# Rows of 1/rms by square root, reciprocal and a Newton step, in place of products with diagonals

## The chip, the cores and the metric

The kernel runs on one core of a Trainium2 chip. The metric is the device time of one execution in microseconds (us). A core has five engines that work at the same time, each through its own queue in order: TensorE (PE, matrix products, and PEld, its weight loads), VectorE (DVE), ScalarE (ACT, activation functions from tables), GpSimd (POOL) and SyncE (SP, which issues transfers). PE writes into PSUM, a memory of eight banks of 512 float32 columns on each of 128 partitions; DVE and ACT read PSUM and the on-chip memory SBUF.

## The reference

One encoder block on 512 tokens of width 1024, in float32. It has three mixers on the normalised input (a bidirectional mLSTM, a neighbourhood attention on a grid, a cross-attention into 256 memory tokens), merged by gates, and a gated convolutional FFN. What matters here is the RMS norm, which stands in three places ahead of products: on x, on mem, and ahead of the FFN.

```python
def rms_norm(x, g):
    xf = x.astype(F32)
    y = xf * lax.rsqrt(jnp.mean(xf * xf, axis=-1, keepdims=True) + EPS)
    return (y * g.astype(F32)).astype(x.dtype)
...
        h = rms_norm(x, mix_norm_g[l])
        proj = h @ w_in[l]
...
        mem_k, mem_v = jnp.split(rms_norm(mem, mem_norm_g[l]) @ w_mem_kv[l], 2, axis=-1)
...
    x = x + merged @ w_out[l]
    x = x + conv_glu_ffn(rms_norm(x, ffn_norm_g[l]), w_ffn_up[l], w_ffn_conv[l], b_ffn_conv[l], w_ffn_down[l])
    return rms_norm(x, final_norm_g)
```

## The kernel before

**Layout.** Activations lie with features on the 128 partitions and tokens along the columns: x is 8 tiles (KT) of 128 x 512. Each float32 operand of a large product is split into two parts of the faster type fp32r, a high part (a rounded copy, made on ACT) and a low part (the rest, made on DVE); a product is then three matmuls (`mm3`, L213 to L215: high by high, high by low, low by high). A projection (`proj`) is 8 x 3 matmuls of 512 columns into one PSUM bank.

**Weights.** They come from memory in blocks. `weights` keeps the transfers (L159, buffers `wr`) three blocks ahead and the splits one block ahead. A block is split in two halves; each has its high part on ACT (L195, `wh`) and its low part on DVE (L196, `wl`). There are four `wh` and four `wl` buffers, so a new half waits until PE has finished with the half four back.

**PSUM.** Two pools of four banks: `mm` for projections, `at` for all else. A projection into a fifth `mm` tile waits for a bank to be read out.

**The norm is applied late.** A projection multiplies the unnormalised input (with the gain g in it); its result is then scaled by 1/rms of each token. Where tokens lie along the columns, that takes a row: 1/rms of all tokens, the same on every partition (`rb`). Where tokens lie on the partitions, it takes a column (`rc`). Both come from the sums of squares: `acc` holds, on each partition, the squares added over the 8 tiles; `two_parts` (L301, L302) splits it; two products with a 128 x 128 tile of ones (L310) give the sum over all features on every partition, so the sums lie there as rows already.

- `rstd_cols` reads the sums with the diagonal of an identity, 128 columns at a time (L314), which gives a column, and takes the power -0.5 on POOL (L317).
- `rstd_row` makes the row from that column: `row_parts` splits the column in two parts (L324, L325) and multiplies the identity by each (L330, eight instructions on DVE for 512 tokens); two products of the ones with these diagonals (L339) spread the values over all partitions, and ACT copies them to `rb` (L341).

**Where they stand.** The order in the queues comes from the order of the code and from the Tile framework, which places the instructions of each engine.

1. *x.* Four projections for the queries (`ps_q`) fill the four `mm` banks; two for the keys (`ps_k`) use `at` banks. The sums and columns are made after the second step of the first key projection, the row after the fifth step of the second. The third key projection needs an `mm` bank; the first one is freed when `conv` has read it: L456 multiplies it by `rb` into `pad`, then follow three steps of a convolution (L458 on ACT, L459 and L460 on DVE) and a tanh (L465).
2. *mem* (256 tokens). Sums and columns after the second of four projections for the output gate (`o`), the row within the fourth. The code around it runs beside the mLSTM, whose steps are interleaved with the projections: Exps on ACT (L710, L714), products on DVE (L715, L717) that make the tiles E, matmuls with E (L725, L727), an Abs on ACT (L729), and gates on the projections (L1027, L1028).
3. *FFN.* The first two projections (`pa`, `pu`) are run up to their last step, which waits for the last tile; the sums stand between the last steps. Two more projections (`pa1`, `pu1`) follow; the row is made after the first step of `pu1`. Then `conv` reads `pa` with the row, and the next projection takes its bank.

Of the kernel before, what the change touches and what calls it, by code (L numbers as in the profile page):

```python
# [31 lines left out]
EPS = 1e-6  # L32
# [78 lines left out]
def hybrid_block(ctx, tc, xg, xT, memT, wflat, vecs, gbias, nabias, outa, outb, outc):  # L111
    nc = tc.nc
    V, A, G, PE, SY = nc.vector, nc.scalar, nc.gpsimd, nc.tensor, nc.sync
# [4 lines left out]
    sp = ctx.enter_context(tc.tile_pool(name="sp", bufs=7))  # L118
    tp = ctx.enter_context(tc.tile_pool(name="tp", bufs=2))
# [6 lines left out]
    def nm(s):  # L126
        uid[0] += 1
        return f"{s}_{uid[0]}"
# [13 lines left out]
    def atps():  # L142
        return atp.tile([P, 512], F32, tag="at", name=nm("at"))
# [4 lines left out]
    st = {"raw": 0, "split": 0}  # L148
# [122 lines left out]
    ident = cp.tile([P, P], F32, name="ident")  # L271
# [3 lines left out]
    onesr = cp.tile([P, P], F32R, name="onesr")  # L275
# [4 lines left out]
    for d in range(2):  # L280
        sgn = 1 if d == 0 else -1
        m = cp.tile([P, P], F32, name=f"msk{d}")
# [5 lines left out]
    for i in range(2):  # L288
        t = cp.tile([P, 514], F32, name=f"pad{i}")
# [9 lines left out]
    def two_parts(acc, ntok):  # L299
        h, l = [sp.tile([P, S], F32R, tag="scr", name=nm("s"))[:, :ntok] for _ in range(2)]  # L300
        A.activation(h, acc, AF.Copy)  # L301
        V.tensor_tensor(l, acc, h.bitcast(F32), op=ALU.subtract)  # L302
        return h, l

    def rstd_cols(parts, ntok, tag, n=D):

        nt = ntok // P
        ps = atps()
        for i in range(2):
            st["mm"] = PE.matmul(ps[:, :ntok], onesr, parts[i], start=i == 0, stop=i == 1).ins  # L310

        v, junk = tiny(nt), scr(P)
        for t in range(nt):
            V.tensor_tensor_reduce(junk, ps[:, t * P:(t + 1) * P], ident, 1.0 / n, EPS, ALU.mult, ALU.add,  # L314
                                   accum_out=v[:, t:t + 1])
        col = cp.tile([P, nt], F32, name=f"rc_{tag}")
        st["pool"] = G.tensor_tensor(col, v, nhalf[:, :nt], op=ALU.pow).ins  # L317
        return col

    def row_parts(col, ntok):  # L320

        nt = ntok // P
        ch, cl = tp.tile([P, 32], F32R, tag="tiny", name=nm("y"), bufs=12)[:, :nt], tiny(nt)
        A.activation(ch, col, AF.Copy)  # L324
        V.tensor_tensor(cl, col, ch.bitcast(F32), op=ALU.subtract)  # L325
        dgs = []
        for c in (ch.bitcast(F32), cl):
            dg = sp.tile([P, S], F32R, tag="scr", name=nm("s"))[:, :ntok]
            for t in range(nt):
                V.tensor_scalar(dg[:, t * P:(t + 1) * P], ident, c[:, t:t + 1], None, op0=ALU.mult)  # L330
            dgs.append(dg)
        return dgs

    def rstd_row(col, ntok, tag, parts=None):

        dgs = parts or row_parts(col, ntok)
        pb = atps()
        for n, dg in enumerate(dgs):
            PE.matmul(pb[:, :ntok], onesr, dg, start=n == 0, stop=n == 1)  # L339
        rb = cp.tile([P, ntok], F32, name=f"rb_{tag}", tag=f"rb{ntok}", bufs=1)  # L340
        A.activation(rb, pb[:, :ntok], AF.Copy)  # L341
        return rb


# [1 line left out]
    XH = [hx[k // 4 * 2][:, (k % 4) * S:(k % 4 + 1) * S] for k in range(KT)]  # L346
    XL = [hx[k // 4 * 2 + 1][:, (k % 4) * S:(k % 4 + 1) * S] for k in range(KT)]
# [3 lines left out]
    ps_k = [atps() for _ in range(2)]  # L351
# [35 lines left out]
    norm = []  # L387
# [7 lines left out]
    def proj(key, XHs, XLs, n=S, at={}, ps=None):  # L395

        ws = weights(key)
        k0 = 0 if ps is None else 1
        if ps is None:
            ps = mmps()  # L400
        for k in range(k0, KT):
            mm3(ps[:, :n], ws[k][0], ws[k][1], XHs[k], XLs[k], k == 0, k == KT - 1)
            if k == 1:
                flush()
            if k in at:
                at[k]()
        return ps
# [32 lines left out]
                mm3(ps_k[f], kh[:, fs], kl[:, fs], XH[0], XL[0], True, False)  # L440

    xsum = two_parts(acc, S)
    proj(("mlk", 0), XH, XL, ps=ps_k[0], at={1: lambda: norm.append(rstd_cols(xsum, S, "x"))})
    proj(("mlk", 1), XH, XL, ps=ps_k[1], at={4: lambda: norm.append(rstd_row(norm[0], S, "x"))})
    rc, rb = norm
    SY.dma_start(gbf, gbias.partition_broadcast(P))
    rcc = cp.tile([P, NT], F32, name="rcc")
    V.tensor_scalar(rcc, rc, C_ML, None, op0=ALU.mult)
# [22 lines left out]
    for f in range(4):  # L471
        ps = ps_k[f] if f < 2 else proj(("mlk", f), XH, XL)
# [27 lines left out]
    for c in range(3):  # L500
        n, nk = TMC[c], TMK[c]
        pss = [(mmps if c % 2 else atps)() for _ in range(NT)]
        for h in range(KT // nk):
            ws = weights(("tm", c, h))
            for t in range(NT):
                tsl = slice(t * P, (t + 1) * P)
                for k in range(nk):
                    kk = nk * h + k
                    ps = pss[t][:, :n]
                    mm3(ps, XH[kk][:, tsl], XL[kk][:, tsl], ws[k][0], ws[k][1], kk == 0, kk == KT - 1)  # L510
        for t in range(NT):
            ps = pss[t]
            if c == 0:
                V.scalar_tensor_tensor(Gt[:, t, :], ps[:, :16], rc[:, t:t + 1], gb, op0=ALU.mult, op1=ALU.add)
            if c < 2:
                o = 16 if c == 0 else 0
# [494 lines left out]
    gens.append(ml_all())  # L1011

    xq = unit()
    mrbs = []
    for f in range(4):
        ps = proj(("xaq", f), XH, XL)
        V.tensor_tensor(xq[:, f * S:(f + 1) * S], ps, rb, op=ALU.mult)
        mem_part(f)
        step(RB)
    for f in range(4):  # L1020
        def mem_row():
            with tc.issue_after(st["mm"]):
                mrbs.append(rstd_row(mrc, M, "m", mparts))

        ps = proj(("o", f), XH, XL, at={1: mem_row} if f == 3 else {})
        t = scr()
        V.tensor_tensor(t, ps, rb, op=ALU.mult)  # L1027
        A.activation(t, t, AF.Tanh, scale=0.5)  # L1028
        if f == 0:
            so.append(unit())  # L1030
            msum = two_parts(macc, M)
        if f == 1:

            with tc.issue_after(st["mm"]):
                mrc = rstd_cols(msum, M, "m")
        if f == 2:
            mparts = row_parts(mrc, M)
        V.tensor_scalar(so[0][:, f * S:(f + 1) * S], t, 1.0, None, op0=ALU.add)
        step(RB)
    mrb = mrbs[0]  # L1040
    mkv = unit()
    mk, mv = mkv[:, 0:1024], mkv[:, 1024:2048]
    for f in range(4):
# [245 lines left out]
    for hh in range(2):  # L1289
        gu = [unit(F32R) for _ in range(6)]  # L1290
        UH = [gu[k // 4][:, (k % 4) * S:(k % 4 + 1) * S] for k in range(HF)]
        UL = [gu[3 + k // 4][:, (k % 4) * S:(k % 4 + 1) * S] for k in range(HF)]
        for j in range(HF):
            f = HF * hh + j
            if f == 0:
                wa, wu = weights(("ua", f)), weights(("uu", f))
                pa, pu = mmps(), mmps()
                for k in range(KT):
                    if k < KT - 1:
                        mm3(pa, wa[k][0], wa[k][1], HH[k], HL[k], k == 0, False)  # L1300
                for k in range(KT - 1):
                    mm3(pu, wu[k][0], wu[k][1], HH[k], HL[k], k == 0, False)
                k = KT - 1
                mm3(pa, wa[k][0], wa[k][1], HH[k], HL[k], False, True)
                rc2 = rstd_cols(two_parts(acc2, S), S, "2")
                mm3(pu, wu[k][0], wu[k][1], HH[k], HL[k], False, True)
                pa1 = proj(("ua", 1), HH, HL)
                norm2 = []
                pu1 = proj(("uu", 1), HH, HL, at={0: lambda: norm2.append(rstd_row(rc2, S, "2"))})
                rb2 = norm2[0]  # L1310
            else:
                pa = pa1 if f == 1 else proj(("ua", f), HH, HL)
            c = conv(pa, rb2, "ffw", "ffb", f, FT)
            sq = scr()
            A.activation(sq, c, AF.Square)
            V.scalar_tensor_tensor(sq, sq, GC, c, op0=ALU.add, op1=ALU.mult)  # L1316
            A.activation(sq, sq, AF.Tanh, scale=GK)  # L1317
            V.scalar_tensor_tensor(c, sq, 1.0, c, op0=ALU.add, op1=ALU.mult)  # L1318
            G.tensor_tensor(c, c, rb2, op=ALU.mult)  # L1319
            if f > 0:  # L1320
                pu = pu1 if f == 1 else proj(("uu", f), HH, HL)
            V.tensor_tensor(c, pu, c, op=ALU.mult)  # L1322
            split_act(UH[j], UL[j], c, 0.5)
        for f in range(KT if hh == 0 else LF - 1):
            ws = weights(("dn", hh, f, 0)) + weights(("dn", hh, f, 1))
            ps = mmps()
            for k in range(HF):
                mm3(ps, ws[k][0], ws[k][1], UH[k], UL[k], k == 0, k == HF - 1)
            V.tensor_tensor(x2[f], ps, x2[f], op=ALU.add)
            if hh == 1:  # L1330
                if f == 0:
                    A.activation(acc3, x2[f], AF.Square)
                else:
                    sq = scr()
                    A.activation(sq, x2[f], AF.Square)
                    G.tensor_tensor(acc3, acc3, sq, op=ALU.add)
# [117 lines left out]
```

## Time and profile before

| | |
|---|---|
| device time, 3 runs | 878.7, 879.12, 879.23 us; median 879.12 |
| profiled execution: span from the first to the last instruction | 878.1 us |
| median of the runs less that span | 1.0 us |
| PE busy | 872.7 us (99%) |
| DVE busy | 582.2 us (66%) |
| ACT busy | 451.4 us (51%) |
| POOL busy | 127.1 us (14%) |
| read from memory, written | 94.80 MB, 4.21 MB |

The profile gives no device time of its own for the profiled execution, only the span. In its lines, "L456 DVE TENSOR_TENSOR pad<-mm,rb_x 128x512 ... x6 | 4.1, 689 | 0.7" names the line of the code, the engine, the operation, the tiles written and read, the shape and the count; then the busy time in us, the mean of one in ns, and the idle time of the engine just before, with what ended it behind an arrow. A timeline has the start and the length in us ahead of these. Matmuls overlap: their listed length runs to the modelled end, and the next one starts earlier. "PEclk" is the clock granted to PE in tenths.

### The profile page before, as it was taken

Reading aid. Unit: us, or ns where it says so; the run is one execution under the profiler, and the core shown is the slowest. Engines: PE = TensorE matmul, PEld = TensorE weight load, DVE = VectorE, ACT = ScalarE, POOL = GpSimd, SP = SyncE. Lnnn points to the kernel's source line nnn. Section 1 sums busy time; section 2 is a strip of 40 time slices with the busy share of each in tenths; the row PEclk is TensorE's granted clock in tenths of the full one; section 3 lists DMA queues with packets and bytes.
Section 4 is the critical chain, followed back from the end, with each engine's and each line's share of the span. In section 5 each row is a group of like instructions: output and inputs, shape, how many; then the busy total and the mean of one; then the engine's idle time right before and its main releaser. Section 6 shows DMA issues by size and latency. Waiting matters only on the chain.

```text
span 878.1 us, 12238 instructions
## 1 busy us (share of the span) xinstructions
PE 872.7 (99%) x4334; PEld 740.4 (84%) x4334; DVE 582.2 (66%) x1211; ACT 451.4 (51%) x953; POOL 127.1 (14%) x203
## 2 busy tenths in 40 slices
PE   9999999999999999999999999999999999999997
PEld 7898889888888888888888888888888888888897
DVE  7694686775667758898676558776633466666433
ACT  7363555754456658888544435444422344444532
POOL 0101100001072460700000002111100011111011
PEclk9999999999999999999999999999999999999999
DMA  8224643522242354533223432222233322222412
GB/s 280 99 73 140 207 135 97 192 85 90 74 137 87 107 146 131 156 110 130 97 97 109 144 107 94 99 97 96 72 103 101 109 97 97 98 97 87 141 34 96
DMA packets 39421, 99.81 MB, mean 114 GB/s; under 512 B 5688, under 2 KB 13880, under 8 KB 39360
## 3 DMA queue, kind: packets, MB, share of 16 engines
q1 hardware_dynamic: 31568, 92.32, 31.1%
q0 software_dynamic: 7360, 6.32, 3.1%
q8 instruction: 34, 0.56, 0.3%
q10 hardware_dynamic: 432, 0.39, 0.1%
q14 instruction: 27, 0.22, 0.1%
HBM read 94.80 MB, written 4.21 MB: 113 GB/s over the span
## 4 chain that ended last, share of the span: by engine, by line
PE 99%; issue 0%; ACT 0%; DVE 0%; POOLq 0%; POOL 0%; DVEq 0%
PE mm L213 29%; PE mm L215 29%; PE mm L214 29%; PE at L214 2%; PE at L213 2%; PE at L215 2%; PE at L872 1%; PE at L725 1%; PE at L853 1%; PE at L727 1%; PE at L690 1%; PE at L834 0%; PE at L835 0%; PE at L706 0%; PE at L960 0%
## 5 line engine op out<-in xcount | busy, mean ns | idle before, releaser
L213 PE MATMUL mm<-u,wh 128*128 128x512 f32 (+1 forms) x1072 | 415.6, 388 | 0.0
L215 PE MATMUL mm<-u,wl 128*128 128x512 f32 (+1 forms) x1072 | 412.2, 385 | 0.0
L214 PE MATMUL mm<-u,wh 128*128 128x512 f32 (+1 forms) x1072 | 411.8, 384 | 0.0
L195 ACT ACTIVATE wh<-wr 128x512 fp32r<-128x512 f32 (+2 forms) x298 | 184.1, 622 | 234.4 <-PE mm L214 188.1
L196 DVE TENSOR_TENSOR wl<-wr,wh 128x512 fp32r<-128x512 f32 (+3 forms) x300 | 203.1, 678 | 92.4 <-ACT wh L195 85.8
L215 PEld LDWEIGHTS mm<-u,wl 128*128 128x128 f32 x1072 | 201.5, 188 | 40.1
L214 PEld LDWEIGHTS mm<-u,wh 128*128 128x128 f32 x1072 | 201.8, 188 | 38.8
L213 PEld LDWEIGHTS mm<-u,wh 128*128 128x128 f32 x1072 | 201.8, 188 | 38.2
L1319 POOL TENSOR_TENSOR s<-s,rb 128x512 f32<-128x512 f32 x22 | 38.3, 1739 | 250.0 <-DVE s L1318 238.1
L538 POOL DMA_DIRECT2D u<-nav_d x128 | 62.2, 512 | 66.5 <-PE at L872 22.5
L219 ACT ACTIVATE u<-s 128x512 fp32r<-128x512 f32 x26 | 16.4, 630 | 57.5 <-DVE s L1322 56.1
L1322 DVE TENSOR_TENSOR s<-mm,s 128x512 f32<-128x512 f32 x22 | 15.2, 691 | 25.1 <-POOL s L1319 25.1
L458 ACT ACTIVATE s<-pad,vec 128x512 f32<-128x512 f32 x30 | 24.4, 813 | 9.5 <-DVE pad L456 9.5
L459 DVE SCALAR_TENSOR_TENSOR s<-pad,vec,s 128x512 f32<-128x512 f32 x30 | 23.6, 786 | 6.1 <-ACT s L458 6.0
L220 DVE SCALAR_TENSOR_TENSOR u<-s,u 128x512 fp32r<-128x512 f32 x26 | 18.0, 691 | 14.1 <-ACT u L219 14.0
L1318 DVE SCALAR_TENSOR_TENSOR s<-s,s 128x512 f32<-128x512 f32 x22 | 15.2, 692 | 13.4 <-ACT s L1317 13.3
L317 POOL TENSOR_TENSOR rc<-y,nhalf 128x4 f32<-128x4 f32 x1 | 1.0, 1032 | 152.9 <-DVE y L314 152.9
L460 DVE SCALAR_TENSOR_TENSOR s<-pad,vec,s 128x512 f32<-128x512 f32 x30 | 22.5, 750 | 0.7
L1317 ACT ACTIVATE s<-s 128x512 f32<-128x512 f32 x22 | 13.9, 632 | 15.1 <-DVE s L1316 15.1
L456 DVE TENSOR_TENSOR pad<-mm,rb 128x512 f32<-128x512 f32 x22 | 15.1, 691 | 7.3 <-PE mm L215 6.5
L213 PE MATMUL mm<-wh,u 128*128 128x512 f32 x48 | 18.9, 394 | 0.0
L214 PE MATMUL mm<-wl,u 128*128 128x512 f32 x48 | 18.8, 392 | 0.0
(315 smaller groups left out, 1028.4 us busy)
## 6 DMA issues: line engine op xcount, KB each, us to landing
wr<-wflat SPq DMA_DIRECT2D x141, 512.0 KB, 3.3
nab<-nabias SPq DMA_DIRECT2D x16, 256.0 KB, 2.7
u<-nav_d POOLq DMA_DIRECT2D x128, 32.0 KB, 2.6
s<-xT SPq DMA_DIRECT2D x15, 256.0 KB, 3.9
wr<-wflat SPq DMA_DIRECT2D x14, 192.0 KB, 2.3
nav_d<-nv POOLq DMA_DIRECT2D x8, 256.0 KB, 2.4
R<-rd SPq DMA_DIRECT2D x8, 256.0 KB, 3.9
wr<-wflat SPq DMA_DIRECT2D x2, 544.0 KB, 3.3
```

The lines of the kernel that those rows point to most:

```text
L195: A.activation(h[:, u:v], src, AF.Copy)
L196: V.tensor_tensor(l[:, u:v], src, h[:, u:v].bitcast(F32), op=ALU.subtract)
L213: PE.matmul(ps, lh, rh, start=start, stop=False)
L214: PE.matmul(ps, lh, rl, start=False, stop=False)
L215: st["mm"] = PE.matmul(ps, ll, rh, start=False, stop=stop).ins
L219: A.activation(h, src, AF.Copy, scale=scale)
L220: V.scalar_tensor_tensor(l, src, scale, h.bitcast(F32), op0=ALU.mult, op1=ALU.subtract)
L458: A.activation(t1, pad[:, 0:512], AF.Identity, scale=vcol(w, i), bias=vcol(b, i))
L459: V.scalar_tensor_tensor(t1, pad[:, 1:513], vcol(w, n + i), t1, op0=ALU.mult, op1=ALU.add)
L460: V.scalar_tensor_tensor(t1, pad[:, 2:514], vcol(w, 2 * n + i), t1, op0=ALU.mult, op1=ALU.add)
L538: G.dma_start(vw[r * 32:(r + 1) * 32, i * 256:(i + 1) * 256], nav_v[hf, r, CW[b]:CW[b] + 32, hp * 256:(hp + 1) * 256])
L1319: G.tensor_tensor(c, c, rb2, op=ALU.mult)
```

## The change

`rstd_cols` is parted: `square_sums` makes the sums by the two products with ones and leaves them in PSUM, and `rstd_cols` takes the column from there as before. `rstd_row` no longer uses the column. It works on the sums themselves, which lie on all partitions: v = sum / n + eps, s = sqrt(v) on ACT, y = 1 / s on DVE, and one Newton step y (1.5 - 0.5 v y y) in three instructions on DVE. The diagonals, their two products and the copy are gone in all three places. The row stands right behind the sums, ahead of the column where one is made; in the FFN no column is made any more.

```diff
-    def rstd_cols(parts, ntok, tag, n=D):
-
-        nt = ntok // P
+    def square_sums(parts, ntok):
+
         ps = atps()
         for i in range(2):
             st["mm"] = PE.matmul(ps[:, :ntok], onesr, parts[i], start=i == 0, stop=i == 1).ins
-
+        return ps
+
+    def rstd_cols(ps, ntok, tag, n=D):
+
+        nt = ntok // P
         v, junk = tiny(nt), scr(P)
...
-    def row_parts(col, ntok):
-
-        nt = ntok // P
-        ch, cl = tp.tile([P, 32], F32R, tag="tiny", name=nm("y"), bufs=12)[:, :nt], tiny(nt)
-        A.activation(ch, col, AF.Copy)
-        V.tensor_tensor(cl, col, ch.bitcast(F32), op=ALU.subtract)
-        dgs = []
-        for c in (ch.bitcast(F32), cl):
-            dg = sp.tile([P, S], F32R, tag="scr", name=nm("s"))[:, :ntok]
-            for t in range(nt):
-                V.tensor_scalar(dg[:, t * P:(t + 1) * P], ident, c[:, t:t + 1], None, op0=ALU.mult)
-            dgs.append(dg)
-        return dgs
-
-    def rstd_row(col, ntok, tag, parts=None):
-
-        dgs = parts or row_parts(col, ntok)
-        pb = atps()
-        for n, dg in enumerate(dgs):
-            PE.matmul(pb[:, :ntok], onesr, dg, start=n == 0, stop=n == 1)
+    def rstd_row(ps, ntok, tag, n=D):
+
+        v, s = scr(ntok), scr(ntok)
         rb = cp.tile([P, ntok], F32, name=f"rb_{tag}", tag=f"rb{ntok}", bufs=1)
-        A.activation(rb, pb[:, :ntok], AF.Copy)
+        V.tensor_scalar(v, ps[:, :ntok], 1.0 / n, EPS, op0=ALU.mult, op1=ALU.add)
+        A.activation(s, v, AF.Sqrt)
+        V.reciprocal(rb, s)
+        V.tensor_tensor(v, v, rb, op=ALU.mult)
+        V.scalar_tensor_tensor(v, v, -0.5, rb, op0=ALU.mult, op1=ALU.mult)
+        V.scalar_tensor_tensor(rb, v, 1.5, rb, op0=ALU.add, op1=ALU.mult)
         return rb
...
-    proj(("mlk", 0), XH, XL, ps=ps_k[0], at={1: lambda: norm.append(rstd_cols(xsum, S, "x"))})
-    proj(("mlk", 1), XH, XL, ps=ps_k[1], at={4: lambda: norm.append(rstd_row(norm[0], S, "x"))})
-    rc, rb = norm
+    def x_norm():
+        ps = square_sums(xsum, S)
+        norm.extend([rstd_row(ps, S, "x"), rstd_cols(ps, S, "x")])
+
+    proj(("mlk", 0), XH, XL, ps=ps_k[0], at={1: x_norm})
+    proj(("mlk", 1), XH, XL, ps=ps_k[1])
+    rb, rc = norm
...
-        def mem_row():
-            with tc.issue_after(st["mm"]):
-                mrbs.append(rstd_row(mrc, M, "m", mparts))
-
-        ps = proj(("o", f), XH, XL, at={1: mem_row} if f == 3 else {})
+        ps = proj(("o", f), XH, XL)
...
             with tc.issue_after(st["mm"]):
-                mrc = rstd_cols(msum, M, "m")
-        if f == 2:
-            mparts = row_parts(mrc, M)
+                mps = square_sums(msum, M)
+            mrb, mrc = rstd_row(mps, M, "m"), rstd_cols(mps, M, "m")
...
-                rc2 = rstd_cols(two_parts(acc2, S), S, "2")
+                rb2 = rstd_row(square_sums(two_parts(acc2, S), S), S, "2")
                 mm3(pu, wu[k][0], wu[k][1], HH[k], HL[k], False, True)
                 pa1 = proj(("ua", 1), HH, HL)
-                norm2 = []
-                pu1 = proj(("uu", 1), HH, HL, at={0: lambda: norm2.append(rstd_row(rc2, S, "2"))})
-                rb2 = norm2[0]
+                pu1 = proj(("uu", 1), HH, HL)
```

More of the change, by code (lines that the diff above doesn't have):

```diff
@@ L1013, in hybrid_block @@
     xq = unit()
-    mrbs = []
     for f in range(4):
@@ L1034, in hybrid_block @@
             with tc.issue_after(st["mm"]):
-                mrc = rstd_cols(msum, M, "m")
-        if f == 2:
-            mparts = row_parts(mrc, M)
+                mps = square_sums(msum, M)
+            mrb, mrc = rstd_row(mps, M, "m"), rstd_cols(mps, M, "m")
         V.tensor_scalar(so[0][:, f * S:(f + 1) * S], t, 1.0, None, op0=ALU.add)
         step(RB)
-    mrb = mrbs[0]
     mkv = unit()
```

## The prediction

> **What bounds the kernel now.** I read the page first: the share of each engine, the granted clock by slice and the chain that ended last.
>
> ```profile
> span 878.1 us, 12238 instructions
> ...
> PE 872.7 (99%) x4334; PEld 740.4 (84%) x4334; DVE 582.2 (66%) x1211; ACT 451.4 (51%) x953; POOL 127.1 (14%) x203
> ...
> PEclk9999999999999999999999999999999999999999
> ...
> PE 99%; issue 0%; ACT 0%; DVE 0%; POOLq 0%; POOL 0%; DVEq 0%
> ```
>
> TensorE (PE) is busy 99% at full clock, and the chain of work that ended last is PE for 99%. Then the waits of PE alone, whose only entry is the start of the program:
>
> ```profile
> PE at L243 <- PEq L1441: 0.8, 1, 0.8
> ```
>
> So a matmul taken away shortens the span by its place in PE's stream, and a wait put in front of PE lengthens it one for one: no later idle time is there to take it back. What a place is worth, and how near PE already is to a wait, shows the timeline around the first row of 1/rms (rb_x):
>
> ```profile
> 36.38 0.62 PE L339 MATMUL at<-s,onesr 128*128 128x512 f32 x2
> 37.03 0.60 ACT L341 ACTIVATE rb_x<-at 128x512 f32<-128x512 f32 x1 [0.73 <-PE at L339]
> 37.66 1.29 DVE L456 TENSOR_TENSOR pad<-mm,rb_x 128x512 f32<-128x512 f32 x2 [0.63 <-ACT rb_x L341]
> 38.42 0.39 PE L214 MATMUL at<-u,wh 128*128 128x512 f32 x1
> 38.65 0.39 PE L215 MATMUL at<-u,wl 128*128 128x512 f32 x1
> 38.65 0.19 PEld L213 LDWEIGHTS mm<-u,wh 128*128 128x128 f32 x1
> 38.88 0.39 PE L213 MATMUL mm<-u,wh 128*128 128x512 f32 x1
> ```
>
> Matmuls of 512 columns start 0.227 us apart (38.42, 38.65, 38.88), though each is listed with 0.39. The first matmul into a new mm bank starts at 38.88. All four mm banks hold q projections until then, and the first is freed by the first "pad" of L456, at 37.66 + 0.69 = 38.35, which needs rb_x. The cover is 0.3 us at the weight load.
>
> **The change part by part.**
>
> *PE, removed:* in each of three places two products with the diagonals (L339).
>
> ```profile
> 139.00 0.40 PE L339 MATMUL at<-s,onesr 128*128 128x256 f32 x2
> ...
> L339 PE MATMUL at<-s,onesr 128*128 128x512 f32 x4 | 1.2, 389 | 0.0
> L339 PE MATMUL at<-s,onesr 128*128 128x256 f32 x2 | 0.4, 280 | 0.0
> ```
>
> Four of 512 columns at 0.227 make 0.91. Two of 256 span 0.40 with 0.28 for one, so they start 0.12 apart: 0.24. Together −1.14 us. The sums themselves (L310) stay.
>
> *New work on the row:* v from PSUM, a square root on ACT, a reciprocal, three Newton steps on DVE. The built program also has six more table loads on ACT, one before each square root and one before the next Tanh or Exp. Nearest rows:
>
> ```profile
> L267 ACT ACT_TABLE_LOAD x1 | 1.3, 1283 | 1.7 <-PEq L1441 1.7
> L465 ACT ACTIVATE s<-s 128x512 f32<-128x512 f32 x8 | 5.0, 629 | 6.3 <-DVE s L460 6.1
> L732 DVE RECIPROCAL y<-y 128x2 f32<-128x2 f32 x16 | 2.6, 163 | 0.3
> L556 DVE RECIPROCAL y<-y 128x32 f32<-128x32 f32 x1 | 0.4, 355 | 0.0
> L456 DVE TENSOR_TENSOR pad<-mm,rb_x 128x512 f32<-128x512 f32 x6 | 4.1, 689 | 0.7 <-ACT rb_x L341 0.6
> ```
>
> v and each Newton step: 0.69, and two such in a row start 0.60 apart (1.29 for the two pads). Root: 0.63. The reciprocal of 512 is nowhere shown. Below: 0.69, as any other elementwise pass. Above: 355/32 = 11.1 ns a column, so 5.68. I take the line through the two rows, (355 − 163)/30 = 6.4 ns a column: 0.163 + 510 × 0.0064 = 3.43, and 1.79 for 256, because it keeps the fixed part that the row of two columns shows.
>
> [...]
>
> *First place (x).* Times are those of before; DVE and ACT take their queues in order.
>
> ```profile
> 29.13 0.62 PE L310 MATMUL at<-s,onesr 128*128 128x512 f32 x2
> ...
> 29.90 0.29 DVE L314 CUSTOM_DVE_ANT_0 s<-at,ident 128x128 f32<-128x128 f32 x1
> ...
> 31.29 1.03 POOL L317 TENSOR_TENSOR rc_x<-y,nhalf 128x4 f32<-128x4 f32 x1 [28.75 <-DVE y L314]
> ...
> 32.35 0.84 DVE L448 TENSOR_SCALAR rcc<-rc_x 128x4 f32<-128x4 f32 x1 [1.15 <-POOL rc_x L317]
> 32.46 0.73 DVE L196 TENSOR_TENSOR wl<-wr,wh 128x512 fp32r<-128x512 f32 x1
> ...
> 39.11 0.62 ACT L195 ACTIVATE wh<-wr 128x512 fp32r<-128x512 f32 x1
> ```
>
> v takes the place of the first reduction: 29.90 to 30.59. The table load waits for v: 30.62 to 31.90; root to 32.56. Meanwhile the reductions and the power of the columns come 0.60 later, so rcc leaves the head of DVE's queue at 33.06, and the reciprocal runs 33.06 to 36.49. Behind it the built program has, on DVE: split of a weight (L196), Newton 1, split, Newton 2, split, Newton 3, split, pad. At 0.60 apart from 36.42 the pad starts at 40.62 and ends at 41.31. PE without its two products would want the bank at 38.43; it gets it at 41.4 and first loads 0.19 of weights, so its matmul starts at 41.6. Stall 3.2 us, in place of a cover of 0.3.
>
> What else stands behind the new waits: on ACT, behind the root, the high halves of two weight splits. The first ran at 30.96 before (it waits for PE's buffers) and now runs at 32.6 to 33.2, in time for its low half, which DVE can take only after the reciprocal anyway (36.42 to 37.1) and which PE wants after 38.9. On POOL, behind the power, only the clearing of mLSTM tiles, 0.6 later and wanted tens of microseconds on. SP's queue isn't passed by anything.
>
> What is late next: PE is 3.2 − 0.45 = 2.75 later than before. The pads are 2.96 later, but a split that stood behind them (0.60) is done already, so DVE is 2.4 later and closes up; the Tanh load fits the 1.56 us that ACT idled before its first Tanh:
>
> ```profile
> 41.29 0.63 ACT L465 ACTIVATE s<-s 128x512 f32<-128x512 f32 x1 [1.56 <-DVE s L460]
> ```
>
> Bounds. With a reciprocal of 5.68 the stall is 3.2 + 2.25 = 5.4. With 0.69 it doesn't vanish: the last split before the pad needs its high half from ACT, whose buffer PE frees only with the last but one matmul of the projection (38.42 above, 37.97 without the products, +0.39 = 38.36). Then 0.63 on ACT (in before it ran at 39.11), 0.60 for the split, 0.69 for the pad, 0.25 to the matmul: 40.6, a stall of 2.2 at least.
>
> *Third place (FFN).* It has more cover:
>
> ```profile
> 519.34 0.63 ACT L195 ACTIVATE wh<-wr 128x512 fp32r<-128x512 f32 x1 [2.03 <-PE mm L214]
> 520.53 0.63 ACT L195 ACTIVATE wh<-wr 128x512 fp32r<-128x512 f32 x1 [0.56 <-PE mm L214]
> ...
> 520.61 0.28 DVE L314 CUSTOM_DVE_ANT_0 s<-at,ident 128x128 f32<-128x128 f32 x1
> ...
> 527.90 1.29 DVE L456 TENSOR_TENSOR pad<-mm,rb 128x512 f32<-128x512 f32 x2 [0.63 <-ACT rb L341]
> ...
> 531.83 0.39 PE L213 MATMUL mm<-u,wh 128*128 128x512 f32 x1
> ```
>
> The next bank is wanted at 531.83, 531.38 without the products. v 520.61 to 521.30; load behind the split of 520.53, to 522.45; root 523.08; reciprocal 526.54; split, Newton, split, Newton, Newton, split, pad end at 530.9, PE could start at 531.1. Stall 0, cover 0.3; with 5.68 it is 2.0. The weights of the projection that runs meanwhile are split before the reciprocal.
>
> *Second place (memory, 256 columns).* No conv waits on this row, but ACT and DVE feed the mLSTM there.
>
> ```profile
> 143.54 0.69 DVE L1027 TENSOR_TENSOR s<-mm,rb_x 128x512 f32<-128x512 f32 x1 [1.54 <-PE mm L215]
> 144.15 0.41 DVE L715 TENSOR_TENSOR E<-E,at 128x256 f32<-128x256 f32 x1
> ...
> 145.11 0.39 PE L725 MATMUL at<-u,E 128*128 128x129 f32 x2
> ```
>
> Before, the E of 144.15 is ready at 144.56 for PE at 145.11. Now ACT loads the root's table after the tanh that ended at 133.70 and has the root (0.38) at 135.3; the reciprocal keeps DVE until 137.1, which moves weight splits by 1.6 that PE wants only after 143. The load for the next Exp stands in ACT's queue right behind the Abs of a chunk (L729, 138.20 before), which waits for PE's products of 137.40 to 137.79 and runs at 137.9. The load is done at 139.3, and the Exps that began at 138.25 begin a good 1.0 later. With the rest of ACT's queue E's factors are complete at about 142; a split and the product of L1027 (143.6) stand ahead of E on DVE, which has it at 144.6. PE's own queue, shorter by 0.24, wants it at 144.85: stall 0, cover 0.2. A reciprocal of 2.84 (256 × 11.1 ns) moves only what is ready before 142 and the last products by up to 1.05: stall 0.9 at most.
>
> ```profile
> 133.07 0.63 ACT L1028 ACTIVATE s<-s 128x512 f32<-128x512 f32 x1 [1.59 <-DVE s L1027]
> ...
> 137.40 0.39 PE L727 MATMUL at<-u,E 128*128 128x129 f32 x2
> 138.20 0.15 ACT L729 ACTIVATE y<-at 128x2 f32<-128x2 f32 x1
> 138.25 0.69 ACT L710 ACTIVATE E<-R,bi 128x128 f32<-128x128 f32 x2
> ...
> 139.43 0.38 ACT L341 ACTIVATE rb_m<-at 128x256 f32<-128x256 f32 x1
> ```
>
> Priced at nothing: the diagonals and small products taken from DVE (L330, L325) and the copies from ACT (L341, L324), because neither engine sets the end there; they are in the walks as room in the queues. The columns of the third place, which aren't made any more, are of that kind too.
>
> **The sum.** −1.14 + 3.2 + 0 + 0 = +2.06 on the span of 878.1: 880.2. The runs shown have a median of 879.12, 1.0 above this span; the time forecast is 879.12 + 2.06 = 881.2. Bounds: −1.14 + 2.2 = +1.06 (880.2) and −1.14 + 5.4 + 2.0 + 0.9 = +7.2 (886.3).
>
> **The rivals.**
> 1. *A short reciprocal, the split as the bound.* If it costs 0.69 to 2.2, the wait for the last weight split decides: 880.2. Against it: both rows of reciprocals grow with columns far beyond what a split does.
> 2. *A table switch that costs more than its load.* The only load in the trace stands at the start, with no activation before it to be finished. If a switch took a second 1.28: first place +0.8 (0.5 of it is hidden behind rcc), third +1.0 beyond its cover, second 2 × 1.28 − 0.2 = +2.3; 881.2 + 4.1 = 885.3. For it: six switches at places with covers of 0.2 to 0.5. [...] Long reciprocals end in the same region.
> 3. *No stall: not slower.* The row is ready before the bank is wanted, so only the six matmuls count: 879.12 − 1.14 = 878.0. It decides if the pad's end comes before 38.2, that is over 3 us earlier than the walk gives and 2.2 before the split that stands ahead of it allows. It holds only if DVE's order on the chip is another than the built one, for which nothing speaks.
>
> **How the numbers follow.** Forecast 0.55 (own range 880.7 to 882.2), rival 1 0.20, rival 2 with long reciprocals 0.20, rival 3 0.05. About 0.2% (1.76 us, to 880.9) can be told from no change. The forecast lies just above that: I put 0.09 of its 0.55 below. Slower 0.46 + 0.20 + 0.02 of rival 1 = 0.68; even rival 3 is only 0.13% faster, so faster 0.02 and within 0.2% the remaining 0.30. The range leaves out most of rival 3 and the upper tail: 879.9 to 885.6.
>
> **What would show it.** In the changed profile: a wait of PE for DVE's pad near 41 us, of about 3.2, and none near 145 and 531; a reciprocal of 512 near 3.4 us; ACT_TABLE_LOAD seven times 1.28, with the square root right behind; PE records down by six. Wrong if PE waits nowhere, if the wait is near 2.2 with a short reciprocal (rival 1), or if waits stand at all three places (rival 2).

## The result, and the profile after

| | before | after |
|---|---|---|
| device time, median of 5 runs | 879.23 us (878.7 to 879.63) | 883.33 us (882.0 to 883.44) |
| ratio, with its 95% interval | | 1.0041 (1.0029 to 1.0053) |
| profiled execution, span | 878.1 us | 881.6 us |

The changed kernel is slower by 0.4%, 4.1 us. Its five runs fall apart into two kinds: three with spans of 881.6 to 881.7 and a mean granted clock of 0.997 or 0.998 (883.33 to 883.44), and two with spans of 880.2 and 880.3 and a clock of 1.0 (882.0 and 882.07). The profiled execution is of the first kind.

The page after: the span, the busy time of the engines, and the chain that ended last, by engine.

```profile
span 881.6 us, 12217 instructions
...
PE 873.2 (99%) x4328; PEld 740.2 (84%) x4328; DVE 592.5 (67%) x1195; ACT 457.7 (52%) x956; POOL 126.3 (14%) x202
...
PE 95%; DVE 3%; issue 1%; ACT 0%; POOL 0%; POOLq 0%; DVEq 0%
```

Six matmuls fewer (4334 to 4328), and yet PE is busy 0.5 us longer; the chain has 3% of DVE in it, where before it was PE alone. PE's waits, in total, times and longest, say where:

```profile
PE mm L213 <- DVE pad L451: 2.5, 1, 2.5
PE at L243 <- PEq L1427: 0.8, 1, 0.8
PE mm L215 <- DVE wl L196: 0.5, 1, 0.5
```

The wait for the first pad at x was forecast. The wait for the low half of a weight split was not. The timeline of ACT, DVE and PE around x (start, length, engine, line):

```profile
30.45 1.28 ACT L328 ACT_TABLE_LOAD   x1 [1.51 <-DVE s L327]
31.74 0.63 ACT L328 ACTIVATE s<-s 128x512 f32<-128x512 f32 x1
...
32.72 0.38 DVE L443 TENSOR_SCALAR rcc<-rc_x 128x4 f32<-128x4 f32 x1 [1.15 <-POOL rc_x L320]
32.80 3.35 DVE L329 RECIPROCAL rb_x<-s 128x512 f32<-128x512 f32 x1
36.06 0.63 DVE L196 TENSOR_TENSOR wl<-wr,wh 128x512 fp32r<-128x512 f32 x1
...
39.61 0.68 DVE L196 TENSOR_TENSOR wl<-wr,wh 128x512 fp32r<-128x512 f32 x1
40.21 1.28 DVE L451 TENSOR_TENSOR pad<-mm,rb_x 128x512 f32<-128x512 f32 x2
...
38.13 0.39 PE L215 MATMUL at<-u,wl 128*128 128x512 f32 x1
41.04 0.76 PE L213 MATMUL mm<-u,wh 128*128 128x512 f32 x1 [2.52 <-DVE pad L451]
41.60 0.63 PE L214 MATMUL mm<-u,wh 128*128 128x512 f32 x1
42.03 0.63 PE L215 MATMUL mm<-u,wl 128*128 128x512 f32 x1
```

The walk is the forecast one: load, root, reciprocal behind rcc, four splits with the three Newton steps between them, pads. PE would have gone on at 38.13 + 0.227 = 38.36 and goes on at 41.04, a stall of 2.68. But then its matmuls start 0.43 apart (41.60, 42.03) in place of 0.227, and are listed with 0.63. Busy time and granted clock by windows show why (the number after POOL's is the clock; of each engine the busy time and the instructions):

```profile
37.00:40.40 3.40, 1.52 (x7) 0.94 (x5) 3.40 (x7) 0.63 (x1) 0.00 (x0) 1.00 0.45 140
40.60:43.80 3.20, 2.76 (x7) 2.21 (x8) 2.79 (x5) 2.48 (x3) 0.00 (x0) 0.50 0.48 168
44.00:46.00 2.00, 2.00 (x10) 1.61 (x10) 1.60 (x4) 1.41 (x3) 0.00 (x0) 1.00 0.00 0
```

From 40.5 to 43.9 PE gets half its clock: seven matmuls in 3.2 us, where ten fit into the next 2.0. That is the 1.4 us by which the two kinds of runs differ, and the reason why PE is busy longer with less to do.

Starts of the same matmul in both profiles make the account (after less before): −0.52 at 36.84 of before, +2.16 at 38.88 (the stall, 2.68), +3.64 at 42.27 (the clock, 1.48), +3.37 at 139.23 (two products of the memory row less), +2.69 at 527.07 (two of the FFN's less, among smaller drifts), +3.30 at 545.89 and +3.44 from there on. This last step, 0.75 in all, is the second wait:

```profile
533.20 1.28 DVE L451 TENSOR_TENSOR pad<-mm,rb 128x512 f32<-128x512 f32 x2
...
541.97 1.79 DVE L454 SCALAR_TENSOR_TENSOR s<-pad,vec,s 128x512 f32<-128x512 f32 x1
...
548.46 0.68 DVE L196 TENSOR_TENSOR wl<-wr,wh 128x512 fp32r<-128x512 f32 x1
...
538.70 1.28 ACT L1303 ACT_TABLE_LOAD   x1
...
548.35 0.39 PE L214 MATMUL mm<-u,wh 128*128 128x512 f32 x1
549.19 0.50 PE L215 MATMUL mm<-u,wl 128*128 128x512 f32 x1 [0.45 <-DVE wl L196]
```

At the FFN the pads came in time for PE's bank, but 5.30 us later than before (527.90), while PE was only 2.69 later. DVE was still behind 15 us afterwards, and only began at 548.46 a split that PE wanted at 548.58. The 1.79 of the row at 541.97, an operation of 0.75 elsewhere, isn't what sets the kernels apart: in both, DVE loses about 1.1 while each of POOL's two products ahead of this split runs (after, 1.79 and 1.78 for 0.75 and 0.68, with POOL's products at 541.60, 1.62 long, and at 545.10, 1.69 long; before, a wait of 1.19 for the one at 534.94, 1.74 long, and 1.78 for 0.75 with the one at 540.54, 1.62 long).

### The profile page after: what moved, and what is told of

The parts are those of the page before. It is cut to its first block, busy times and chain, and to the rows that moved or that the text cites. A ratio compares the mean times of both kernels' runs of the same rounds, so it can differ in the third digit from the quotient of the medians.

```text
span 881.6 us, 12217 instructions
## 1 busy us (share of the span) xinstructions
PE 873.2 (99%) x4328; PEld 740.2 (84%) x4328; DVE 592.5 (67%) x1195; ACT 457.7 (52%) x956; POOL 126.3 (14%) x202
## 4 chain that ended last, share of the span: by engine, by line
PE 95%; DVE 3%; issue 1%; ACT 0%; POOL 0%; POOLq 0%; DVEq 0%
PE mm L213 28%; PE mm L215 28%; PE mm L214 28%; PE at L214 1%; PE at L213 1%; PE at L215 1%; PE at L867 1%; PE at L720 1%; PE at L848 1%; PE at L722 1%; PE at L685 1%; DVE wl L196 1%; PE at L829 0%; PE at L830 0%; PE at L701 0%
## 5 line engine op out<-in xcount | busy, mean ns | idle before, releaser
L213 PE MATMUL mm<-wh,u 128*128 128x512 f32 x48 | 18.9, 394 | 0.0
L1315 DVE TENSOR_TENSOR u<-mm,u 128x512 f32<-128x512 f32 x13 | 9.0, 692 | 14.6 <-PE mm L215 14.6
L215 PE MATMUL mm<-wh,u 128*128 128x512 f32 x48 | 18.7, 390 | 0.0
```

What stands on the lines that cost most here:

```text
L213: PE.matmul(ps, lh, rh, start=start, stop=False)
L215: st["mm"] = PE.matmul(ps, ll, rh, start=False, stop=stop).ins
```

## The experiments

All times are of the run named; "before" is the kernel before in runs of the same sessions, whose spans have a median of 877.5 us. Line numbers differ between the kernels.

### Where the loss sits: x as before, and x alone

```diff
-    def x_norm():
-        ps = square_sums(xsum, S)
-        norm.extend([rstd_row(ps, S, "x"), rstd_cols(ps, S, "x")])
-
-    proj(("mlk", 0), XH, XL, ps=ps_k[0], at={1: x_norm})
-    proj(("mlk", 1), XH, XL, ps=ps_k[1])
-    rb, rc = norm
+    proj(("mlk", 0), XH, XL, ps=ps_k[0], at={1: lambda: norm.append(rstd_cols(square_sums(xsum, S), S, "x"))})
+    proj(("mlk", 1), XH, XL, ps=ps_k[1], at={4: lambda: norm.append(old_row(norm[0], S, "x"))})
+    rc, rb = norm
```

> Row for x made as before (columns, diagonals, two products), the new row only for the 256 memory positions and for the FFN. Theory (the loss is a PE stall at x of 2.7 us, a clock cut behind it of 1.35 us, and a late weight split in the FFN of 0.6 us): no PE wait for DVE's pad, granted clock 1.00 in every run, the FFN's wait of PE L215 for wl of about 0.5 still there; span 878.1 - 0.24 - 0.45 + 0.6 = 878.0. Rival A (the whole loss sits at x, the FFN wait comes only from the shifted timing): no FFN wait, span 877.4. Rival B (the lower clock has nothing to do with the stall): some runs still at 0.997 with spans 1.4 apart. Rival C (table switches cost beyond their loads): span 879 or more.

Measured: 879.41 us, ratio 1.0002 (0.9993 to 1.0011), spans 877.1 to 878.1 with a median of 877.6, clock 0.999 or 1.0 in all eleven. No wait for a pad; the FFN's wait for wl was there with 0.5. So the FFN's loss stands by itself (against rival A), with the new row in the other two places the spans stay below the 879 of rival C, and with x as before the clock is never cut.

The counterpart has the new row at x only, and the diagonals of before (`old_row`) for the memory and the FFN:

```diff
-            mrb, mrc = rstd_row(mps, M, "m"), rstd_cols(mps, M, "m")
+                mrc = rstd_cols(square_sums(msum, M), M, "m")
...
-                rb2 = rstd_row(square_sums(two_parts(acc2, S), S), S, "2")
+                rc2 = rstd_cols(square_sums(two_parts(acc2, S), S), S, "2")
...
+                pu1 = proj(("uu", 1), HH, HL, at={0: lambda: norm2.append(old_row(rc2, S, "2"))})
```

> New row only for x; the rows for the memory positions and the FFN as before. Theory: PE waits about 2.5 us for the pad at 41 us, span 878.1 - 0.45 + 2.7 = 880.3 where the clock stays at 1.00 and 881.7 where it is cut behind the stall; no FFN wait for wl. Rival A: as the theory at x, but with the FFN wait of 0.5 still there, span 880.9 or 882.3. Rival C (the switches of the other two places cost too): span 879.5 or less.

Measured: 883.24 us, ratio 1.0043 (1.0029 to 1.0057); spans 881.0 to 881.5 at a clock of 0.997 or 0.998 in four runs, 880.4 at 0.999 in one. PE's waits:

```profile
PE mm L213 <- DVE pad L475: 2.6, 1, 2.6
PE at L243 <- PEq L1460: 0.8, 1, 0.8
```

The row at x alone makes as much loss as the whole change: what the other two rows save (0.69) the FFN's wait takes back.

### What cuts the clock: filling the stall, and lengthening it

Ten products whose result nobody uses, in PE's queue where it stalls; and the same with four:

```diff
     proj(("mlk", 1), XH, XL, ps=ps_k[1])
+    fill = atps()
+    with tc.issue_after(st["mm"]):
+        for _ in range(10):
+            PE.matmul(fill, onesr, XH[0], start=True, stop=True)
```

> The changed kernel with ten more 512-column products (result unused) in PE's queue between the second key projection and the next product, 10 x 0.227 = 2.27 us in the place of the stall. Theory (the clock is cut because PE stood idle for 2.7 us): granted clock 1.00 in every run, left-over wait for the pad about 0.4, span 880.2 in every run, 1.4 less than the cut runs of the changed kernel. Rival B (the lower clock has nothing to do with the stall): some runs still at 0.997 and 881.6. Rival D (the ten products delay something else, the weight splits' buffers for instance): span above 880.5 at clock 1.00.

Measured: spans 879.7 to 880.5, median 880.1, clock 0.999 or 1.0 in all five; 881.91 us, ratio 1.0032 (1.0019 to 1.0044). The wait that was left for the pad was 0.2. The same windows as above, of this kernel:

```profile
37.00:40.40 3.40, 3.40 (x15) 2.43 (x13) 3.40 (x7) 0.64 (x1) 0.00 (x0) 1.00 0.47 164
40.60:43.80 3.20, 3.20 (x14) 2.65 (x15) 2.78 (x5) 2.88 (x4) 0.00 (x0) 1.00 0.44 164
```

The products that matter start as late as without the filling (at 40.59 in this run, whose PE stands 0.45 ahead of the changed kernel's from its first microseconds on, and at 41.04 there), yet PE runs at 1.00 behind it: work for nothing made the kernel 1.4 us faster than its median. Rival B falls, and rival D too: no span is above 880.5.

> The changed kernel with four unused 512-column products in the stall in place of ten: PE idle 2.68 - 0.91 = 1.8. Span 880.2 where the clock stays at 1.00, 881.6 where it is cut. Theory (the cut needs a certain length of idle time, which 2.7 reaches only in some runs): no run cut, 880.2 in all. Rival I (any idle stretch of over a microsecond can cut it, by chance): some runs at 0.997 or 0.998 and 881.6.

Measured: seven runs with spans 879.8 to 880.3, clock 0.999 or 1.0 in all; 881.83 us, ratio 1.0029 (1.0018 to 1.004). The wait for the pad was 1.6, and no run was cut. Rival I is not borne out.

The other way, the reciprocal at x made twice:

```diff
         V.reciprocal(rb, s)
+        if tag == "x":
+            V.reciprocal(rb, s)
```

> The changed kernel with the reciprocal at x made twice: the stall grows from 2.7 by 3.27, less the one or two splits that the built order now puts behind the pads, to about 5.4. Theory (PE's idle time brings the clock cut, likelier the longer it lasts): clock at 0.997 or lower in every run, with a cut stretch as in the changed kernel or longer, span 880.2 + 2.7 + 1.4 = 884.3 at least. Rival B (the cut is unrelated to the length of the stall): about half of the runs uncut, at 882.9.

Measured: 886.94 us, ratio 1.0087 (1.007 to 1.0104), spans 884.9, 885.1, 885.1 and 886.1, clock 0.996 or 0.997 in all four runs. The built order kept all four splits ahead of the pads, so PE's wait was 5.8 and not 5.4. The clock by windows:

```profile
38.00:43.20 5.20, 0.20 (x1) 0.00 (x0) 5.17 (x7) 0.63 (x1) 0.00 (x0) 1.00 0.32 107
43.40:49.80 6.40, 5.76 (x14) 4.54 (x15) 4.70 (x7) 4.07 (x5) 0.00 (x0) 0.50 0.27 82
50.40:52.00 1.60, 1.60 (x8) 1.31 (x7) 1.57 (x4) 0.73 (x2) 0.00 (x0) 1.00 0.00 0
```

PE resumed at 44.04 and ran at half clock for 6.1 us more. So the cut comes with the length of the idle time: in all 4 runs with 6.0 us of it; in 9 of the 19 with the 2.7 us stall (3 of 5 of the changed kernel, 4 of 5 with x alone, 2 of 9 of the runs below that alter the FFN); in none of the 12 with ten or four products filled in, and in none of the 55 of the kernels here whose wait at x is gone or nearly gone. What the traces show of runs with the same stall, with and without a cut, stands in the last section.

### The floor under the stall

At x the reciprocal is left out and a product stands in its place:

```diff
-        V.reciprocal(rb, s)
+        if tag == "x":
+            V.tensor_tensor(rb, s, s, op=ALU.mult)
+        else:
+            V.reciprocal(rb, s)
```

> At x alone the reciprocal is replaced by an elementwise product (the reciprocal there is left out), 3.35 us to about 0.7 on DVE. Theory (the last weight split of the second key projection, whose buffer PE gives back with its last but one group, stands ahead of the pad and sets the floor): the stall shrinks only from 2.7 to about 2.1, span 879.6 at clock 1.00. Rival E (the row's own chain decides alone): the stall shrinks by 2.66 to nothing, span 877.6. If the clock is cut after 2.1 us too, spans are 1 us or more above these.

Measured: spans 876.6 to 877.4, median 877.1; 878.91 us, ratio 0.9996 (0.9987 to 1.0004); no wait for a pad at all. The theory missed; the missing stall is rival E's, and the span is near its 877.6. DVE and PE in the timeline:

```profile
35.53 0.69 DVE L335 SCALAR_TENSOR_TENSOR rb_x<-s,rb_x 128x512 f32<-128x512 f32 x1
36.14 0.68 DVE L196 TENSOR_TENSOR wl<-wr,wh 128x512 fp32r<-128x512 f32 x1
36.74 1.28 DVE L454 TENSOR_TENSOR pad<-mm,rb_x 128x512 f32<-128x512 f32 x2
...
39.04 0.69 DVE L196 TENSOR_TENSOR wl<-wr,wh 128x512 fp32r<-128x512 f32 x1
```

The split that was to set the floor now stands behind the pads (39.04). When the kernel was built with another operation in the row, the framework ordered DVE's queue anew. The floor was a property of one built order, not of the dependences. The reciprocal's 3.35 us decides the stall in this kernel, together with what its length does to the order, which this run does not part.

### What leaves DVE behind in the FFN

Tiny activations on two constant columns call for tables early, so that the 1.28 us load falls where ACT has nothing ready: for the square root behind ACT's copy of the square sums, for Tanh behind the row's own root.

```diff
+    def load(fn, ins):
+
+        with tc.issue_after(ins):
+            return A.activation(tiny(2), ones[:, :2], fn).ins
...
+                h2 = two_parts(acc2, S)
+                load(AF.Sqrt, st["cp"])
-                rb2 = rstd_row(square_sums(two_parts(acc2, S), S), S, "2")
+                rb2 = rstd_row(square_sums(h2, S), S, "2")
+                load(AF.Tanh, st["root"])
```

> The changed kernel; in the FFN alone two tiny activations call for the tables early: a square root of two constant columns right behind ACT's copy of the square sums, and a Tanh right behind the row's own root, so that both loads (1.28 each) fall where ACT has nothing ready. Theory (the FFN's wait of 0.5 for a weight split comes from the row that ends late and from the Tanh load in the conv's chain; DVE carries that backlog for 15 us): the pad comes 1.3 earlier, the wait of PE L215 for wl is gone, spans 0.6 below the changed kernel's, 881.0 with the clock cut behind the x stall and 879.6 without; the x stall itself as before at 2.5. Rival F (the backlog comes from DVE's own work, the reciprocal above all, or from POOL beside it, not from the loads): the wait stays within 0.2 of 0.5.

Measured: 881.03 us, ratio 1.0025 (1.0014 to 1.0037); spans 878.8 to 879.4 in the five runs at a clock of 1.0, 880.7 and 881.0 in two at 0.998. PE's waits:

```profile
PE mm L213 <- DVE pad L456: 2.5, 1, 2.5
PE at L243 <- PEq L1435: 0.8, 1, 0.8
```

The wait for wl is gone. Behind the row PE's starts stay level with before's (+0.88 at 527.07, and no step behind it), where the changed kernel lost 0.75. Rival F falls: DVE has the same reciprocal and the same two losses beside POOL here (1.19 idle, and 1.78 for 0.75). A call for each table alone, in one execution each:

> In the FFN only the square root's table is called for early, the Tanh load stays where it was. If the late row is what leaves DVE behind, the wait of PE L215 for wl (0.5) is gone with the pad 1.3 earlier; if the Tanh load in the conv's chain is, it stays at about 0.5; if each second of delay counts alike, it is gone here and in the next run, since 1.28 is more than 0.5.

> In the FFN only the Tanh table is called for early, right behind the row's root; the root's own load stays on the row's path. If the late row is what leaves DVE behind, the wait of 0.5 for wl stays; if the Tanh load is, it goes; if both count alike, it goes.

Measured: with the root's table early no wait for wl (span 879.3, clock 1.0); with the Tanh early 0.2 is left of it (span 879.4, clock 1.0):

```profile
PE mm L215 <- DVE wl L196: 0.2, 1, 0.2
```

Both delays count, the late row somewhat more; taking either away is nearly enough. The built order of DVE changed in both, too, so the shares are not exact.

### Versions without the stall

The same early load at x, and rcc behind the row in DVE's queue (with the two calls in the FFN):

```diff
     xsum = two_parts(acc, S)
+    load(AF.Sqrt, st["cp"])
...
-    V.tensor_scalar(rcc, rc, C_ML, None, op0=ALU.mult)
+    with tc.issue_after(st["row"]):
+        V.tensor_scalar(rcc, rc, C_ML, None, op0=ALU.mult)
```

> As the run before, and at x the same early call for the square root's table, with rcc put behind the row in DVE's queue. Theory: the reciprocal at x starts at about 31.1 in place of 32.8, the two splits of the fourth key block fall behind the pads in the built order, pads start at about 38.4 in place of 40.2; PE's wait there shrinks from 2.5 to about 0.6, the clock is 1.00 in every run, span 880.2 - 2.0 - 0.6 = 877.6, about level with the kernel before (877.5). Rival G (a load called for early holds up ACT's weight copies as long as it did the root): stall still 2 or more, span 879 or more.

Measured: 878.75 us, ratio 0.9995 (0.9986 to 1.0004); spans 876.5 to 877.8, median 876.9, clock 0.999 or 1.0 in all eleven. The reciprocal started at 30.02 and the pads at 36.74, the wait at x was 0.2. This execution's PE stands 1.1 ahead of the changed kernel's from its start on, so on that kernel's time the reciprocal starts at 31.1, as expected, and the pads at 37.9, 0.5 earlier than expected. Rival G falls. The wait is smaller than the 0.6 expected, and the median 0.7 below the 877.6.

Next, the root read the sums in PSUM (`A.activation(s, ps[:, :ntok], AF.Sqrt, scale=1.0 / n, bias=eps)`), and the columns stood behind the row:

> As the run before, and the root reads the sums in PSUM itself (scale 1/n, bias eps), beside the v that only the Newton step now needs, and the four column reductions stand behind the row in DVE's queue. Theory (the stall at x is nothing but the row's chain on ACT and DVE): pads start at about 37.4, PE waits for at most 0.2, clock 1.00 in every run, no wait in the FFN; span 877.5 - 1.14 = 876.4, ratio to the kernel before about 0.9987. Rival H (the column reductions moved late hold up what uses rc and rcc, or the splits put behind the pads come late for the third key block): a new PE wait between 41 and 60, span 877 or more.

Measured: 879.12 us, ratio 0.9999 (0.999 to 1.0008), spans 877.0 to 878.0, median 877.4. A miss: v waited 0.81 behind ACT's read of the same sums, so the reciprocal came no earlier against PE's own stream than in the version before, the built order put three splits ahead of the row's end, and PE lost 0.6 at the pad. (The profile puts 0.46 of it to a copy on ACT that ended at 38.53. The first pad ended at 38.40, and the matmul starts at 38.55, 0.15 behind it, as after the pad in the changed kernel.)

Last, in the version before that, the low half of one split is made behind the first two pads:

```diff
-                V.tensor_tensor(l[:, u:v], src, h[:, u:v].bitcast(F32), op=ALU.subtract)
+                if key == ("mlk", 2) and a > 0:
+                    st["later"] = (l[:, u:v], src, h[:, u:v].bitcast(F32))
+                else:
+                    V.tensor_tensor(l[:, u:v], src, h[:, u:v].bitcast(F32), op=ALU.subtract)
...
+        if f == 1:
+            with tc.issue_after(st["pad"]):
+                l, src, h = st["later"]
+                V.tensor_tensor(l, src, h, op=ALU.subtract)
```

> As the run e7_tables, and the DVE half of one weight split (the second half of the third key block, which PE wants 2.7 us after the pads) stands behind the first two pads in DVE's queue in place of ahead of them. Theory (what is left of the x stall, 0.3, is DVE work ahead of the pads): pads start 0.6 earlier, no PE wait there, none in the FFN, clock 1.00 in every run; only the six products' 1.14 is left, span 877.5 - 1.14 = 876.4, ratio to the kernel before about 0.9987. Rival (the moved split is wanted sooner than it is made): a wait of PE for wl of 0.3 or more between 38 and 44, span 876.9 or more.

Measured: 878.58 us against 879.43 of the kernel before in the same session, ratio 0.9992 (0.9983 to 1.0001); spans 876.5 to 877.6, median 876.8, clock 0.999 or 1.0 in all eleven. DVE and PE at x, and PE's waits:

```profile
30.55 3.35 DVE L337 RECIPROCAL rb_x<-s 128x512 f32<-128x512 f32 x1 [0.22 <-ACT s L336]
...
36.71 1.29 DVE L461 TENSOR_TENSOR pad<-mm,rb_x 128x512 f32<-128x512 f32 x2
...
37.55 0.39 PE L218 MATMUL at<-u,wl 128*128 128x512 f32 x1
37.78 0.39 PE L216 MATMUL mm<-u,wh 128*128 128x512 f32 x1
```

```profile
PE at L246 <- PEq L1445: 0.8, 1, 0.8
PE at L216 <- DVE pad L461: 0.2, 1, 0.2
```

The matmul into the new bank starts 0.23 behind the last one: no stall. What is left is a later wait for a pad at 53.6, around which PE's starts lose about 0.5 against before's; the two versions ahead of this one have it too. So of the 1.14 saved some 0.8 arrives. It is the best of the versions, but its interval still reaches 1: all that the change can bring is about what a measurement of this kernel can tell.

## Why the prediction was right or wrong

The direction was right and for the reason given: the row at x comes too late for the bank, and PE stalls there. The time was 2.1 us too low (881.2 against 883.33): the clock cut adds 1.4 and the FFN's wait 0.75, which were not forecast, the stall was 0.5 shorter than forecast, and some 0.4 is not assigned. The forecast's own range, 880.7 to 882.2, misses the measured time. That the wide range, 879.9 to 885.6, holds it is luck: its upper part was put there for a long reciprocal and for table switches that cost more than their loads, and neither was seen. By its steps:

- *PE, removed, −1.14.* It holds: 4328 matmuls; PE's starts (after less before) go from −0.12 to −0.52 at x, from +3.64 to +3.37 at the memory and from +3.11 to +2.69 at the FFN, 1.09 in all; and e12, freed of the stalls, has a span 0.7 to 0.9 below before's with about 0.5 of a later wait in it.
- *New work on the row.* The reciprocal took 3.35 us for 512 columns and 1.75 for 256, against 3.43 and 1.79 by the line through the two short rows: right.
- *First place, stall 3.2.* Measured 2.68. Here only the size was off: DVE's walk to the pads ran 0.4 ahead of the forecast (pads at 40.21, not 40.62), and the matmul followed the pads' start by 0.83, not 0.98.
- *"A wait put in front of PE lengthens it one for one."* This step failed. In the three cut runs the stall cost 1.4 us more than its length, and the median is one of those. The forecast read the clock of before as a constant, though no idle time in that trace could test it. The experiments show that the stall brings the cut: filled, it is gone (e3_fill, e9_fill4), doubled, it is there in all four runs (e6_long).
- *"With 0.69 it doesn't vanish ... a stall of 2.2 at least."* Wrong: without the reciprocal there was no stall (e4_no_recip). The walk held DVE's order fixed while it changed a duration that sets the order.
- *Third place, stall 0, cover 0.3.* Right for the bank that the walk ended at (no wait there), wrong for the stage: the walk stopped at the pad and did not ask what DVE, 2.6 us later than PE's stream, owes PE next. That was a weight split, 15 us on, and 0.75. At x the same question was asked ("closes up"), and there it held.
- *Second place, stall 0.* Right: PE waits for nothing there, and gains its 0.24.
- *Rival 2, a table switch beyond its load.* Not seen. All seven loads after took 1283 ns, as the only one of before did, and no run shows a second cost of a switch, which this rival put at another 1.28. A load began 0.02 behind the end of the activation ahead of it, and the root 0.02 behind the load (timeline of ACT at the memory row, after):

```profile
136.87 0.63 ACT L1018 ACTIVATE s<-s 128x512 f32<-128x512 f32 x1 [1.60 <-DVE s L1017]
137.52 1.28 ACT L328 ACT_TABLE_LOAD   x1
138.82 0.42 ACT L328 ACTIVATE s<-s 128x256 f32<-128x256 f32 x1
```

- *The base.* The sum stood on the profiled span of 878.1. That doesn't touch the time, which adds the change to the median of the runs, but spans are compared with it. Later runs of the kernel before have a median of 877.5; by its eighth microsecond that execution stands 0.1 to 1.25 us behind those of all the other kernels. The changed kernel's two runs at full clock are 2.7 above the 877.5; the measured terms, −1.14 + 2.68 + 0.75, give +2.3. The other 0.4 is not assigned to a cause: runs of one kernel scatter by as much.

## What to carry to other kernels

When TensorE is busy 99% and a change makes it wait, price the wait by its length and by the clock afterwards (2.7 us of waiting cost 1.4 us more in three of five runs here), and fill part of the wait if it can't be avoided (four unused products were enough here: clock 0.999 or 1.0 in all seven runs). Walk each moved stage until the late engine has caught up, not only to the first thing that is wanted; and treat the order of a framework's queue as one more result of the change, since other durations give another order. Here it paid to give an elementwise row its tables before its input was there: in the FFN the wait of 0.5 was gone (e5_ffn_tables), and at x, with rcc moved behind the row as well, the wait of 2.5 shrank to 0.2 (e7_tables).

## What the runs showed of the hardware

Only the clock was not expected. The cut lasted from 40.49 to 43.91 after (clock 0.73 in the 0.2 us window at either end, 0.50 between), from 41.62 to 45.03 with x alone, and from 43.33 to 50.16 with the doubled reciprocal (worked out in the same way): 3.42, 3.41 and 6.83 us, the last being twice the others. Its start has no fixed distance to the stall: after, it lies 0.55 ahead of PE's resuming, with x alone 1.1 behind it. And a stall of 2.7 us doesn't always bring it: it did in 9 of 19 runs.

The traces let the place of the cuts be set against the start of the program. After, PE's starts of 512 columns are 0.43 apart just before 6.36 and 0.23 just behind (the clock column of the profile reads 1.00 on both sides), and the cut at 40.49 lies 34.13 behind this point, ten times 3.41. With x alone the point is at 4.07, and the cut lies 37.55 behind it, eleven times 3.41. In e5, e10 and e11, whose traces show the same stall (a wait of 2.5) without a cut, it is at 5.10, 5.98 and 4.96. A period is called here a stretch of 3.41 us, the length of the cuts, counted on from that point; these are the periods around the stall (the length, then PE's busy time). First the ones ahead of the cut, after and with x alone:

```profile
37.08:40.49 3.41, 1.44 (x7) 0.86 (x5) 3.41 (x7) 0.63 (x1) 0.00 (x0) 1.00 0.47 148
38.20:41.62 3.42, 1.08 (x5) 0.95 (x6) 3.07 (x6) 1.39 (x3) 0.00 (x0) 1.00 0.68 228
```

Then the two periods that share the stall in e5, in e10 and in e11:

```profile
35.82:39.23 3.41, 2.22 (x10) 1.50 (x8) 3.41 (x7) 0.63 (x1) 0.00 (x0) 1.00 0.29 70
39.23:42.65 3.42, 2.09 (x9) 1.77 (x10) 3.04 (x5) 2.10 (x2) 0.00 (x0) 1.00 0.71 229
36.70:40.11 3.41, 1.59 (x8) 0.98 (x6) 3.41 (x7) 0.63 (x1) 0.00 (x0) 1.00 0.43 137
40.11:43.52 3.41, 2.70 (x12) 2.30 (x13) 2.99 (x5) 2.43 (x3) 0.00 (x0) 1.00 0.54 181
35.68:39.09 3.41, 2.15 (x10) 1.45 (x8) 3.41 (x7) 0.63 (x1) 0.00 (x0) 1.00 0.23 64
39.09:42.51 3.42, 2.15 (x10) 1.80 (x11) 3.04 (x5) 2.10 (x2) 0.00 (x0) 1.00 0.73 253
```

PE was idle for 1.97 and 2.34 us of a period where the clock was cut behind it, and for 1.82 at most where it wasn't (e10, 3.41 less 1.59). The other kernels fit: 1.60 in one period with four products filled in, no cut; with the doubled reciprocal 1.72 in the period from 36.50, no cut, and all of the next one, cut. There the clock stayed at half for a second period, though PE was idle for only 0.71 us of the first one at half clock (it resumed at 44.04); after, with 0.55 of it, the clock was full again. That what counts is how much of the stall falls into one period is the author's estimate from these seven traces: no run moved the stall against the period, the other runs left no trace, and no experiment shows it.
